# A LayerNorm between two halves of a projection: summing its squares once, and inside blocks of products

## The chip, the cores and the metric

The kernel runs on one core of a Trainium2 chip. Its time is the time of one execution on the device in microseconds (us). A core has a matrix engine (TensorE, PE in the profile; PEld is its weight load), VectorE (DVE), ScalarE (ACT), GpSimd (POOL) and SyncE (SP), each with a queue of instructions of its own that it works off in order, and DMA engines that move data beside them. Engines wait for each other through semaphores.

## The reference

One residual block over 512 positions of width 1024, in fp32:

```python
h = h + 0.5 * _swiglu(_rmsnorm(h, ffn1_norm[i]), ffn1_w_in[i], ffn1_w_out[i])
z = _rmsnorm(h, mix_norm[i]) @ w_in[i]
...
y_conv = _conv_module(conv_a, conv_gt, conv_w[i], conv_b[i], conv_ln_g[i], conv_ln_b[i])
y_gla = _gla(q, k, v, r, g_lr, gate_w_up[i], gate_b[i], gla_norm[i])
h = h + jnp.concatenate([y_conv, y_gla], axis=-1) @ w_out[i]
h = h + 0.5 * _swiglu(_rmsnorm(h, ffn2_norm[i]), ffn2_w_in[i], ffn2_w_out[i])
...
```

The convolution module multiplies `a` by sigmoid(`b`), runs a causal convolution of width 31 on each of 512 channels, and then normalizes over the channels:

```python
mu = jnp.mean(xf, axis=-1, keepdims=True)
var = jnp.mean(jnp.square(xf - mu), axis=-1, keepdims=True)
y = (xf - mu) * lax.rsqrt(var + EPS)
return (y * g.astype(jnp.float32) + b.astype(jnp.float32)).astype(x.dtype)
```

followed by SiLU. The change touches this LayerNorm and the product with `w_out` around it.

## The kernel before, in words

**Layout.** Activations lie transposed: 128 channels on the partitions, 512 positions along a row. The model's 1024 channels are eight such tiles `hT[0..7]`, the convolution's 512 channels four, `acc[0..3]` (named `cv` in the profile).

**Products.** An fp32 number is split into a high part of the type `F32R` and the rest, of the same type. A product of two such numbers is three matmuls, high by high, high by low, low by high (`mm3`, line 216). Weights come in by `load` (line 171, SyncE's queue) into one of two raw buffers (`wr`), and are split in one of two ways. `high` (line 178) casts the high part on ScalarE, and `low` (line 188) subtracts it from the raw weight on VectorE. `added` (line 193) does the low part without VectorE: its two lines are:

```python
act.mul(l3, r3, -1.0)
pool.dma_start(out=l3.bitcast(F32), in_=r3, accum_op=ALU.add)
```

Here `l3` and `r3` are the tiles that the profile names `wl` (or `wa`) and `wr`; the multiplication writes the negated weight rounded to the high part's precision, and a DMA issued from GpSimd's queue adds the raw weight to it. `wh` is the high part.

**The output projection.** It has eight blocks of 128 output channels, n = 0 to 7, and each block sums over eight input tiles `mix[k]`: k = 0 to 3 from the convolution (`yc`), k = 4 to 7 from the attention (`yg`). `first_part(n, w)` (line 882) does the twelve products of k = 4 to 7 of a block, which do not need the convolution; `part` (line 876) does either half. `part` can take a dictionary `mid` that calls a function ahead of the products of some k.

**The stretch that the change rewrites** (lines 945 to 979). Blocks 0 and 1 come first, then `taps(124)` issues what is left of the convolution's steps on VectorE (each multiplies a shifted row by a column of weights and adds it; with two tiles left, they alternate), then the last two weights, blocks 6 and 7, are split with `added`. Blocks 4 and 5 follow, then the last two of four products with the constant matrix `mean`, which put the mean over the channels into a PSUM tile `mub` (named `ax`). After block 2 VectorE subtracts the mean from each `acc[c]`, ScalarE squares it (`lnsq`), and 16 small products with a column of ones sum the squares of all four tiles into one column per 128 positions (`ax<-ones,lnsq`). `rsqrt_mean` (line 251) makes 1/sqrt of it with an operation `ms` on VectorE, a power on GpSimd, the optional function `between`, and four small operations on VectorE (`rs`). Block 3 follows; then `spread` (line 267) multiplies the columns with the identity so that the factor stands on all 128 partitions (`ax<-ident,rs`). Each tile is then multiplied by it on VectorE (`yc`), goes through SiLU with gain and bias on ScalarE, and is split by `split` (line 154): a cast on ScalarE (`ycH`), a subtraction on VectorE (`ycL`). Block 6 is issued last, and from there the loop over k adds the convolution's half to blocks 0 to 2, then to 3 to 6. Block 7 comes behind, and the second FFN.

**What sets the order.** All engine calls go through the class `Ordered` (line 36), so that nearly all instructions carry line 46 in the profile. While it is on, each of the three engines TensorE, VectorE and ScalarE gets its instructions in the order in which the code issues them; after `in_order(False)` a scheduler may move them. The stretch above is under the fixed order up to the loop over k. Raw buffers, PSUM banks (`bank`, seven; `aux`, one) and the tiles of `bt` come from pools that rotate; a new tile waits for the readers of the tile whose place it takes.

Of the kernel before, what the change touches and what calls it, by code (L numbers as in the profile page):

```python
# [8 lines left out]
F32 = mybir.dt.float32  # L9
# [6 lines left out]
P = 128  # L16
# [46 lines left out]
def block_kernel(ctx: ExitStack, tc: tile.TileContext, a: dict, out: bass.AP):  # L63
# [24 lines left out]
    def bt(dt=F32, s="a"):  # L88
        return big.tile([P, SEQ], dt, tag="A", bufs=NA, name=nm(s))
# [10 lines left out]
    def aux():  # L100
        return pp.tile([P, SEQ], F32, tag="aux", bufs=1, name=nm("ax"))
# [91 lines left out]
    def added(w):  # L193

        h3, l3, r3 = w
        act.mul(l3, r3, -1.0)
        pool.dma_start(out=l3.bitcast(F32), in_=r3, accum_op=ALU.add)
        return w
# [52 lines left out]
    def rsqrt_mean(ss, n, w, bufs=3, between=None):  # L251

        ms = tmp("ms", 16)[:, :w]
        dve.tensor_scalar(ms, ss, 1.0 / n, EPS, ALU.mult, ALU.add)
        r = tmp("rs0", 16)[:, :w]
        pool.tensor_tensor(out=r, in0=ms, in1=negh[:, :w], op=ALU.pow)
        if between is not None:
            between()
        t = tmp("rs1", 16)[:, :w]
        dve.tensor_tensor(out=t, in0=r, in1=r, op=ALU.mult)  # L260
        dve.tensor_tensor(out=t, in0=t, in1=ms, op=ALU.mult)
        dve.tensor_scalar(t, t, -0.5, 1.5, ALU.mult, ALU.add)
        rs = tmp(f"rs{bufs}", 16, bufs=bufs)[:, :w]
        dve.tensor_tensor(out=rs, in0=r, in1=t, op=ALU.mult)
        return rs
# [275 lines left out]
    def taps(n):  # L541

        for _ in range(n):
            if not conv:
                return
            i = turn[0] % min(2, len(conv))
            turn[0] += 1
            try:
                next(conv[i])
            except StopIteration:  # L550
                conv.pop(i)
# [317 lines left out]
    def ohigh(n):  # L869
        return (high4 if n in (4, 5) else high)(raw_o[n - n % 2][:, :, (n % 2) * P:(n % 2 + 1) * P])  # L870
# [5 lines left out]
    def part(ps, w, ks, first, last, mid={}):  # L876
        for k in ks:
            if k in mid:
                mid[k]()
            mm3(ps, *rows_of(w, k), *mix[k], first and k == ks[0], last and k == ks[-1])  # L880

    def first_part(n, w):
        ps = bank()
        part(ps, w, range(4, 8), True, False)
        half[n] = (w, ps)

    oload(0)
# [56 lines left out]
        nc.sync.dma_start(out=ptok[t], in_=a["p"][0, 0, t * P:(t + 1) * P, :])  # L944
    first_part(0, wo[0])
    first_part(1, wo[1])
    taps(124)
    for n in (6, 7):
        wo[n] = added(ohigh(n))
    first_part(4, wo[4])  # L950
    first_part(5, wo[5])
    for c in range(2, 4):
        pe.matmul(mub, mean, acc[c], start=False, stop=(c == 3))
    first_part(2, wo[2])
    sqs = []
    for c in range(4):
        dve.tensor_tensor(out=acc[c], in0=acc[c], in1=mub, op=ALU.subtract)
        sq = bt(s="lnsq")
        act.activation(sq, acc[c], AF.Square)
        sqs.append(sq)  # L960
    ssl = aux()[:, 0:TB]
    for c in range(4):
        for j in range(TB):
            pe.matmul(ssl[:, j:j + 1], sqs[c][:, j * P:(j + 1) * P], ones,
                      start=(c == j == 0), stop=(c == 3 and j == TB - 1), skip_group_check=True)
    rln = rsqrt_mean(ssl, D_CONV, TB)
    first_part(3, wo[3])
    rln = spread(rln, copy=False)
    yc = []
    for c in range(4):  # L970
        t = bt(s="yc")
        dve.tensor_tensor(out=t, in0=acc[c], in1=rln, op=ALU.mult)
        act.activation(t, t, AF.Silu, bias=vec("conv_ln_b", c), scale=vec("conv_ln_g", c))
        yc.append(t)
        if c == 2:
            mix[0] = split(yc[0], "yc")
    for c in range(1, 4):
        mix[c] = split(yc[c], "yc")
    first_part(6, wo[6])


    norm = Norm()
# [130 lines left out]
```

## Time and profile before

| | us |
|---|---|
| median of 3 runs | 998.3 (998.11 to 998.40) |
| profiled execution | 998.15 |
| its span in the trace | 996.4 |
| TensorE busy in the span | 978.2 (98%) |
| VectorE, ScalarE, GpSimd busy | 528.0, 355.4, 36.2 |
| mean granted clock of TensorE | 0.992 |

Times in the trace count from the start of the span. A row of the timeline gives start, length, engine, line, operation, output and inputs, the tile's shape, and how many such instructions it merges; in brackets stands how long the engine was idle before it, and for whom it waited. Matmuls overlap in a pipeline, so that a dense one is recorded with 0.39 us while the next starts 0.23 us later. A product of plain fp32 numbers (with `ones`, `ident` or `mean`) stands as two records.

### The profile page before, as it was taken

What the parts mean: (1) busy time and instruction counts of PE and PEld (TensorE: products, weight loads), DVE (VectorE), ACT (ScalarE), POOL (GpSimd) and SP (SyncE); (2) the same over time, 40 slices, a digit from 0 to 9 for tenths busy, and PEclk for the clock granted to TensorE, in tenths of its full rate; (3) what the DMA queues carried; (4) which work ended last, traced back from release to release, by engine and by line L of the source; (5) the groups of instructions that cost most, each with busy time, mean ns of one, the idle gap of its engine ahead of it and who ended that gap; (6) DMA issues with size and microseconds to landing.
All of it is one profiled execution on the core that took longest, in us unless ns stands there. A gap on an engine that the chain in (4) does not pass through costs nothing.

```text
span 996.4 us, 11226 instructions
## 1 busy us (share of the span) xinstructions
PE 978.2 (98%) x4594; PEld 807.1 (81%) x4594; DVE 528.0 (53%) x750; ACT 355.4 (36%) x541; POOL 36.2 (4%) x46
## 2 busy tenths in 40 slices
PE   7999999999999999999998999999999999999996
PEld 5888888888888888788877888888888888888885
DVE  4654334444434566999982844444333444345454
ACT  5633213232223343463654623322222232233442
POOL 1000000000000000001231000000000000000000
PEclk9999999999999999999997999999999999999998
DMA  5633223223422421125687223222233222233212
GB/s 171 196 125 107 85 86 118 93 85 105 149 85 80 131 85 43 42 85 128 128 130 144 78 99 121 85 83 87 95 116 127 87 85 80 69 100 111 85 43 85
DMA packets 99624, 100.53 MB, mean 101 GB/s; under 512 B 3331, under 2 KB 93013, under 8 KB 99572
## 3 DMA queue, kind: packets, MB, share of 16 engines
q1 hardware_dynamic: 90592, 93.93, 29.4%
q0 software_dynamic: 8800, 5.77, 4.5%
q8 instruction: 36, 0.59, 0.3%
q10 hardware_dynamic: 180, 0.12, 0.0%
q14 instruction: 16, 0.13, 0.0%
HBM read 92.46 MB, written 2.10 MB: 95 GB/s over the span
## 4 chain that ended last, share of the span: by engine, by line
PE 95%; DMA 2%; ACT 1%; SPq 0%; DVE 0%; issue 0%; POOLq 0%; DVEq 0%; ACTq 0%
PE ps L46 94%; PE ax L46 2%; DMA wr<-in_w_out 1%; DMA x<-in_x 1%; DMA wr<-in_ffn_w_in 0%; ACT wl L46 0%; ACT wh L46 0%; ACT ygH L46 0%; SPq L150 0%; ACT yc L46 0%; DVE yc L46 0%; ACT hgH L46 0%; POOLq L1109 0%; DVE m L46 0%; ACT lnsq L46 0%
## 5 line engine op out<-in xcount | busy, mean ns | idle before, releaser
L46 ACT CAST wh<-wr 128x1024 fp32r<-128x1024 f32 (+2 forms) x174 | 172.0, 992 | 452.6 <-PE ps L46 418.9
L46 PE MATMUL ps<-hgH,wh 128*128 128x512 f32 x752 | 293.4, 390 | 0.0
L46 PE MATMUL ps<-hgL,wh 128*128 128x512 f32 x752 | 292.9, 390 | 0.0
L46 PE MATMUL ps<-hgH,wl 128*128 128x512 f32 x752 | 292.9, 389 | 0.0
L46 DVE TENSOR_TENSOR wl<-wr,wh 128x1024 fp32r<-128x1024 f32 (+2 forms) x166 | 189.8, 1146 | 61.5 <-ACT wh L46 61.3
L46 PEld LDWEIGHTS ps<-hgH,wh 128*128 128x128 f32 x752 | 141.3, 188 | 29.9 <-issue 0.8
L46 PEld LDWEIGHTS ps<-hgH,wl 128*128 128x128 f32 x752 | 141.2, 188 | 29.3
L46 PEld LDWEIGHTS ps<-hgL,wh 128*128 128x128 f32 x752 | 141.3, 188 | 29.1
L46 PE MATMUL ps<-actL,wh 128*128 128x512 f32 x352 | 137.2, 390 | 0.0
L46 PE MATMUL ps<-actH,wl 128*128 128x512 f32 x352 | 137.1, 389 | 0.0
L46 PE MATMUL ps<-actH,wh 128*128 128x512 f32 x352 | 136.9, 389 | 0.0
L46 DVE TENSOR_TENSOR u<-ps,bc 128x512 f32<-128x512 f32 x48 | 33.2, 691 | 131.1 <-PE ps L46 131.1
L46 DVE SCALAR_TENSOR_TENSOR cv<-glu,cw,cv 128x504 f32<-128x504 f32 (+25 forms) x120 | 81.2, 732 | 0.6
L46 DVE TENSOR_TENSOR g<-ps,bc 128x512 f32<-128x512 f32 x48 | 33.1, 691 | 86.0 <-PE ps L46 83.1
L46 PEld LDWEIGHTS ps<-actL,wh 128*128 128x128 f32 x352 | 66.1, 188 | 13.9 <-DVE actL L46 0.2
L46 PEld LDWEIGHTS ps<-actH,wh 128*128 128x128 f32 x352 | 66.1, 188 | 13.7
L46 PEld LDWEIGHTS ps<-actH,wl 128*128 128x128 f32 x352 | 66.1, 188 | 13.6
L46 DVE SCALAR_TENSOR_TENSOR h<-ps,h 128x512 f32<-128x512 f32 x40 | 27.7, 692 | 89.1 <-PE ps L46 89.1
L46 PE MATMUL ps<-wh,hgH 128*128 128x512 f32 (+1 forms) x136 | 52.4, 385 | 0.0
L46 PE MATMUL ps<-wl,hgH 128*128 128x512 f32 (+1 forms) x136 | 51.8, 381 | 0.0
L46 PE MATMUL ps<-wh,hgL 128*128 128x512 f32 (+1 forms) x136 | 51.3, 377 | 0.0
L46 ACT ACTIVATE s<-g 128x512 f32<-128x512 f32 x48 | 30.3, 632 | 40.2 <-DVE g L46 35.5
(189 smaller groups left out, 783.8 us busy)
## 6 DMA issues: line engine op xcount, KB each, us to landing
wr<-in_ffn_w_in SPq DMA_DIRECT2D x42, 1024.0 KB, 5.1
wr<-in_w_in SPq DMA_DIRECT2D x10, 1024.0 KB, 5.0
wr<-in_ffn_w_out SPq DMA_DIRECT2D x12, 768.0 KB, 4.6
wr<-in_ffn_w_out SPq DMA_DIRECT2D x8, 1024.0 KB, 5.1
wr<-in_ffn_w_out SPq DMA_DIRECT2D x8, 640.0 KB, 6.8
wl<-wr POOLq DMA_DIRECT2D x8, 512.0 KB, 8.9
wr<-in_w_out SPq DMA_DIRECT2D x4, 1024.0 KB
wr<-in_ple_w_gate SPq DMA_DIRECT2D x8, 512.0 KB, 3.5
```

What stands on the lines that cost most here:

```text
L46: inst = call(*args, **kwargs)
```

## The change

It does five things in the stretch described. The rest of the convolution is issued tile by tile and no longer alternating. The last two products with `mean` stand apart, one behind block 4 and one behind block 5. The four squares are added on VectorE into one tile, and four products with the column of ones sum that. The weights of blocks 6 and 7 are cast behind the squares, and their low parts made by VectorE (`low`) and no longer by ScalarE and a DMA: that of block 6 while GpSimd computes the power, that of block 7 behind the last part of the convolution. The column sum stands inside block 3 (ahead of its products of k = 7), the spreading inside block 6 (at the same place), and each tile's SiLU is followed at once by its cast.

```diff
-    def first_part(n, w):
+    def first_part(n, w, mid={}):
         ps = bank()
-        part(ps, w, range(4, 8), True, False)
+        part(ps, w, range(4, 8), True, False, mid)
         half[n] = (w, ps)
...
     first_part(0, wo[0])
     first_part(1, wo[1])
-    taps(124)
-    for n in (6, 7):
-        wo[n] = added(ohigh(n))
+    for steps in list(conv):
+        for _ in steps:
+            pass
+    conv.clear()
     first_part(4, wo[4])
+    pe.matmul(mub, mean, acc[2], start=False, stop=False)
     first_part(5, wo[5])
-    for c in range(2, 4):
-        pe.matmul(mub, mean, acc[c], start=False, stop=(c == 3))
+    pe.matmul(mub, mean, acc[3], start=False, stop=True)
     first_part(2, wo[2])
-    sqs = []
+    sqs, lln, yc = [], [], []
     for c in range(4):
         dve.tensor_tensor(out=acc[c], in0=acc[c], in1=mub, op=ALU.subtract)
         sq = bt(s="lnsq")
         act.activation(sq, acc[c], AF.Square)
         sqs.append(sq)
-    ssl = aux()[:, 0:TB]
-    for c in range(4):
-        for j in range(TB):
-            pe.matmul(ssl[:, j:j + 1], sqs[c][:, j * P:(j + 1) * P], ones,
-                      start=(c == j == 0), stop=(c == 3 and j == TB - 1), skip_group_check=True)
-    rln = rsqrt_mean(ssl, D_CONV, TB)
-    first_part(3, wo[3])
-    rln = spread(rln, copy=False)
-    yc = []
-    for c in range(4):
-        t = bt(s="yc")
-        dve.tensor_tensor(out=t, in0=acc[c], in1=rln, op=ALU.mult)
-        act.activation(t, t, AF.Silu, bias=vec("conv_ln_b", c), scale=vec("conv_ln_g", c))
-        yc.append(t)
-        if c == 2:
-            mix[0] = split(yc[0], "yc")
+    for n in (6, 7):
+        wo[n] = ohigh(n)
+
     for c in range(1, 4):
-        mix[c] = split(yc[c], "yc")
-    first_part(6, wo[6])
+        dve.tensor_tensor(out=sqs[0], in0=sqs[0], in1=sqs[c], op=ALU.add)
+
+    def ln_sums():
+        lln.append(rsqrt_mean(colsum([sqs[0]]), D_CONV, TB, between=lambda: low(wo[6])))
+
+    def ln_out():
+        rln = spread(lln[0], copy=False)
+        for c in range(5):
+            if c < 4:
+                t, hi, lo = bt(s="yc"), bt(F32R, "ycH"), bt(F32R, "ycL")
+                dve.tensor_tensor(out=t, in0=acc[c], in1=rln, op=ALU.mult)
+                act.activation(t, t, AF.Silu, bias=vec("conv_ln_b", c), scale=vec("conv_ln_g", c))
+                act.copy(hi, t)
+                mix[c] = hi, lo
+                yc.append(t)
+            if c:
+                hi, lo = mix[c - 1]
+                dve.tensor_tensor(out=lo, in0=yc[c - 1], in1=hi.bitcast(F32), op=ALU.subtract)
+        low(wo[7])
+
+    first_part(3, wo[3], {7: ln_sums})
+    first_part(6, wo[6], {7: ln_out})
```

The order of instructions shows it at three places. The first is ScalarE between the weights of block 3 (`wh_3885`, `wl_3886`) and the SiLUs (`yc`), before:

```order
L46 CAST wh_3885<-wr_3729 128x1024
L46 ACTIVATE wl_3886<-wr_3729 128x1024
L46 CAST wh_3936<-wr_3890 128x1024
L46 ACTIVATE wl_3937<-wr_3890 128x1024
L46 CAST wh_3941<-wr_3890 128x1024
L46 ACTIVATE wl_3942<-wr_3890 128x1024
L46 ACTIVATE lnsq_3988<-cv_2667 128x512
L46 ACTIVATE lnsq_3991<-cv_2668 128x512
L46 ACTIVATE lnsq_3994<-cv_2669 128x512
L46 ACTIVATE lnsq_3997<-cv_2670 128x512
L46 ACTIVATE yc_4044<-yc_4044,vcol 128x512
L46 ACTIVATE yc_4047<-yc_4047,vcol 128x512
```

and of the change:

```order
L46 CAST wh_3885<-wr_3729 128x1024
L46 ACTIVATE wl_3886<-wr_3729 128x1024
L46 ACTIVATE lnsq_3978<-cv_2667 128x512
L46 ACTIVATE lnsq_3981<-cv_2668 128x512
L46 ACTIVATE lnsq_3984<-cv_2669 128x512
L46 ACTIVATE lnsq_3987<-cv_2670 128x512
L46 CAST wh_3989<-wr_3890 128x1024
L46 CAST wh_3992<-wr_3890 128x1024
L46 ACTIVATE yc_4042<-yc_4042,vcol 128x512
L46 CAST ycH_4043<-yc_4042 128x512
L46 ACTIVATE yc_4048<-yc_4048,vcol 128x512
```

The four instructions on raw buffer `wr_3890` (blocks 6 and 7) have become two and stand behind the squares, and each SiLU has its cast behind it. The second place is TensorE from the last products of block 2 (`ps_3974` before, `ps_3964` in the change) to the start of block 3 (`ps_4026`, `ps_3998`), before:

```order
L46 MATMUL ps_3974<-ygL_3878,wh_3880 128x512
L46 MATMUL ps_3974<-ygH_3876,wl_3881 128x512
L46 MATMUL ax_3999<-ones,lnsq_3988 128x1 x4
L46 MATMUL ax_3999<-ones,lnsq_3991 128x1 x4
L46 MATMUL ax_3999<-ones,lnsq_3994 128x1 x4
L46 MATMUL ax_3999<-ones,lnsq_3997 128x1 x4
L46 MATMUL ps_4026<-ygH_3864,wh_3885 128x512
L46 MATMUL ps_4026<-ygL_3866,wh_3885 128x512
L46 MATMUL ps_4026<-ygH_3864,wl_3886 128x512
```

and of the change:

```order
L46 MATMUL ps_3964<-ygH_3876,wl_3881 128x512
L46 MATMUL ps_3998<-ygH_3864,wh_3885 128x512
L46 MATMUL ps_3998<-ygL_3866,wh_3885 128x512
L46 MATMUL ps_3998<-ygH_3864,wl_3886 128x512
L46 MATMUL ps_3998<-ygH_3868,wh_3885 128x512
L46 MATMUL ps_3998<-ygL_3870,wh_3885 128x512
L46 MATMUL ps_3998<-ygH_3868,wl_3886 128x512
L46 MATMUL ps_3998<-ygH_3872,wh_3885 128x512
L46 MATMUL ps_3998<-ygL_3874,wh_3885 128x512
L46 MATMUL ps_3998<-ygH_3872,wl_3886 128x512
L46 MATMUL ax_4008<-ones,lnsq_3978 128x1 x4
L46 MATMUL ps_3998<-ygH_3876,wh_3885 128x512
```

Block 3 now follows block 2 directly, with its low weight `wl_3886` in the third product, and the column sum stands behind nine of its products. The third place is VectorE from the end of the additions of squares to the first multiplication by the factor, in the change alone (before, the five small operations stood without the split between them):

```order
L46 TENSOR_TENSOR lnsq_3978<-lnsq_3978,lnsq_3987 128x512
L46 TENSOR_SCALAR ms_4013<-ax_4008 128x4
L46 TENSOR_TENSOR wl_3990<-wr_3890,wh_3989 128x1024
L46 TENSOR_TENSOR rs_704_4018<-rs_703_4015 128x4
L46 TENSOR_TENSOR rs_704_4018<-rs_704_4018,ms_4013 128x4
L46 TENSOR_SCALAR rs_704_4018<-rs_704_4018 128x4
L46 TENSOR_TENSOR rs_705_4022<-rs_703_4015,rs_704_4018 128x4
L46 TENSOR_TENSOR yc_4042<-cv_2667,ax_4037 128x512
```

The split of block 6's weight (`wl_3990`) stands behind `ms`, which reads the column sum, and ahead of the four operations that finish the factor.

## The prediction

> **What bounds the kernel now.** I read the page first (TensorE busy 98% of the 996.4 us), then the chain of work that ended last. From 542 us on it is TensorE alone up to the tail; around the change, from 512 to 542 us, it leaves TensorE:
>
> ```profile
> 512.66 9.47 DMA wr<-in_w_out
> ...
> 522.15 0.75 ACT wh L46
> ...
> 523.11 1.05 ACT wl L46
> 524.16 0.93 ACT wh L46
> 525.09 0.96 ACT wl L46
> 526.05 0.53 ACT lnsq L46
> ...
> 526.62 6.99 PE ax L46 x32
> 533.61 4.34 PE ps L46 x12
> 537.95 0.91 PE ax L46 x8
> ...
> 538.88 0.70 DVE yc L46
> ...
> 541.83 0.52 ACT ycH L46
> ...
> 542.39 19.35 PE ps L46 x84
> ...
> 585.14 0.79 PE ax L46 x8
> ...
> 591.01 345.26 PE ps L46 x1525
> ```
>
> Columns are start, length, what. Four ScalarE instructions on the last output weights (`wh`, `wl`, 522.15 to 526.05), which waited for their DMA, stand ahead of the squares `lnsq`. The 16 column-sum products (32 records, two each) then take 6.99 us; four of the same kind later take 0.79 us. A dense product costs 19.35/84 = 0.230 us. I call 542.39, where the first product with the convolution's result (`ycH`) starts, H0: behind it TensorE waits for nothing until the tail, so what moves H0 moves the end. TensorE's timeline and stretches of 1 us (columns: stretch, length, busy time of PE, PEld, DVE, ACT, POOL, granted clock, DMA share, GB/s):
>
> ```profile
> 519.05 1.88 PE L46 MATMUL ax<-cv,mean 128*128 128x512 f32 x4
> ...
> 523.31 0.39 PE L46 MATMUL ps<-ygH,wl 128*128 128x512 f32 x1
> 526.62 6.99 PE L46 MATMUL ax<-ones,lnsq 128*128 128x1 f32 x32 [2.93 <-ACT lnsq L46]
> ...
> 534.47 0.63 PE L46 MATMUL ps<-ygH,wl 128*128 128x512 f32 x1
> 534.89 0.63 PE L46 MATMUL ps<-ygH,wh 128*128 128x512 f32 x1
> ```
>
> ```profile
> 526.00:527.00 1.00, 0.38 (x2) 0.38 (x2) 0.00 (x0) 1.00 (x4) 0.56 (x1) 0.72 0.41 46
> 527.00:528.00 1.00, 1.00 (x6) 1.00 (x6) 0.00 (x0) 1.00 (x3) 1.00 (x1) 0.50 1.28 143
> ...
> 536.00:537.00 1.00, 1.00 (x4) 0.77 (x4) 0.00 (x0) 0.00 (x0) 0.00 (x0) 0.67 1.38 174
> ...
> 988.00:989.00 1.00, 0.41 (x4) 0.20 (x2) 0.55 (x3) 0.55 (x2) 0.00 (x0) 1.00 0.39 150
> ...
> 990.00:991.00 1.00, 0.00 (x0) 0.00 (x0) 0.50 (x2) 0.44 (x2) 0.23 (x1) 0.82 0.00 0
> ```
>
> TensorE idles 2.93 us, and its clock falls to 0.50 at 526.44 (a share of 0.72 means 0.44 us of full speed in that microsecond) and is back at 536.66 (share 0.67). While it is down a dense product costs 0.42 to 0.43 (534.47 to 534.89) and a column-sum record 6.99/32 = 0.218 instead of 0.79/8 = 0.099. In the tail the last product ends at 988.41 and the clock falls at 990.64. The distances, 10.22 and 453.98 us, are 3 and 133 steps of 3.41 us, so I take the clock to be decided on that grid: 523.03, 526.44, 529.85, 533.27, 536.68. The windows in which it fell held TensorE work of about 0.7 of 3.41 us (to the end of the product at 523.31) and, in the tail, 988.41 - 987.23 = 1.2. Column sums did not bring it back; one window of dense products (533.27 to 536.68) did.
>
> **The change, part by part.** *One sum instead of four, at full clock:* 16 products become 4. *Squares ahead of the weights:* the subtractions of the mean start at 520.97, as before; the mean's products are only spread between two blocks, and convolution block 3 still ends at 519.00, ahead of them:
>
> ```profile
> 510.03 8.97 DVE L46 SCALAR_TENSOR_TENSOR cv<-glu,cw,cv 128x510 f32<-128x510 f32 x12
> 520.97 2.48 DVE L46 TENSOR_TENSOR cv<-cv,ax 128x512 f32<-128x512 f32 x4 [1.96 <-PE ax L46]
> 533.64 0.16 DVE L46 TENSOR_SCALAR ms<-ax 128x4 f32<-128x4 f32 x1 [10.20 <-PE ax L46]
> ...
> 534.96 0.16 DVE L46 TENSOR_TENSOR rs<-rs 128x4 f32<-128x4 f32 x1 [1.15 <-POOL rs L256]
> ...
> 535.56 0.16 DVE L46 TENSOR_TENSOR rs<-rs,rs 128x4 f32<-128x4 f32 x1
> ...
> 554.88 0.68 DVE L46 TENSOR_TENSOR sqacc<-sqacc,sq 128x512 f32<-128x512 f32 x1
> ...
> 558.75 1.22 DVE L46 TENSOR_TENSOR wl<-wr,wh 128x1024 fp32r<-128x1024 f32 x1
> ```
>
> ```profile
> 522.15 1.05 ACT L46 CAST wh<-wr 128x1024 fp32r<-128x1024 f32 x1 [9.27 <-DMA wr<-in_w_out]
> ...
> 525.96 2.17 ACT L46 ACTIVATE lnsq<-cv 128x512 f32<-128x512 f32 x4
> ...
> 543.69 0.82 ACT L46 ACTIVATE yc<-yc,vcol 128x512 f32<-128x512 f32 x1 [1.36 <-DVE yc L46]
> ```
>
> ScalarE was idle for 9.27 us before 522.15, so each square (2.17/4 = 0.54) follows its subtraction (2.48/4 = 0.62), the last ends at 524.1. The three added additions on VectorE (0.68 each, like `sqacc`, of which some 0.6 is the step) end at 523.45 + 1.9 = 525.35. ScalarE casts `wh` of blocks 6 and 7 behind the squares, 524.1 to 526.1, with the raw load there since 522.13. The two `wl` multiplications and two GpSimd DMAs go away; two splits of 1.22 us on VectorE take their place.
>
> *What is late next.* With the sums ready at 525.35, TensorE comes to block 3 at 523.54, right behind block 2, ten microseconds sooner than before (533.61). Its third product reads `wl` of block 3, and that weight is still built by an accumulating DMA:
>
> ```profile
> 513.17 1.55 POOL L197 DMA_DIRECT2D wl<-wr  x1 [0.34 <-ACT wl L46]
> ```
>
> ```profile
> wl<-wr POOLq DMA_DIRECT2D x1, 512.0 KB, 13.2
> ...
> wl<-wr POOLq DMA_DIRECT2D x1, 512.0 KB, 12.2
> ```
>
> ```profile
> 526.52 12.64 SPq L174 DMA_DIRECT2D wr<-in_ffn_w_in  x2
> ```
>
> This DMA (the first landing row) lands 13.2 us after its issue, at 526.4; SyncE's next load, which needs the raw buffer it reads, is issued at 526.52 and confirms it. Nothing that the change removes ran on the queues before: the two DMAs that go away follow the `wl` multiplications, which ended at 524.16 and 526.05. So the new order meets a wait that lay hidden: TensorE does two products, to 524.0, and idles until 526.45. This is an order in TensorE's queue, so block 3's other products and the column sum behind them wait too. The price: 2.45 us of idle where 2.93 stood. For a bound, the next such DMA took 12.2 us (second landing row), 1.0 us less; 13.2 was the longest of those around, so I take no later end.
>
> *The clock.* On the grid, window 523.03 to 526.44 would hold 1.0 to 1.1 us of TensorE work, between the two that let the clock fall (0.7 and 1.2). I take it that it falls again, at 526.44, and comes back at 529.85 since that window is filled by dense products (seven at 0.43 = 3.0 us).
>
> *The sum.* Seven products at 0.427 from 526.45: 529.44. Column sum: two records at 0.218, at 529.85 the clock returns, six at 0.10: 530.47. Three products of block 3 and two of block 6: 531.6. The third product of block 6 needs its `wl`: that split stands on VectorE behind `ms`, which waits for the column sum, so it runs from 530.66 (0.16 + hand-over) to 531.90; TensorE loses 0.35. The power on GpSimd runs beside the split (533.80 to 534.96 with its hand-overs before); the four small `rs` operations are queued behind the split, 0.8 us (534.96 to 535.72 before), ready at 532.7 and hidden. Seven products more: 531.95 + 1.6 = 533.54. Spreading (0.91, as at 537.95): 534.45. From there to H0: multiplication 0.70, SiLU 0.82, cast 0.60 (0.52 in the chain and its start-up), 0.15 of hand-overs (0.02 to 0.05 between rows) = 2.27 against 3.54 before (538.85 to 542.39), where three SiLUs went ahead of the first cast. H0 = 536.72, of which 0.69 is covered by block 6's last three products.
>
> 542.39 - 536.72 = 5.67 us gained. Behind H0 the convolution's next parts are needed after nine to twelve products each, 2.1 us or more apart, and made every 1.4 (a multiplication and a subtraction on VectorE, a SiLU and a cast on ScalarE), so no further wait; block 7's split is done some 6 us after H0 and used behind the 84 products, 19 us after. Profiled execution 998.15 us (span 996.4 and 1.75 around it), 0.15 under the median of the runs: 998.15 - 5.67 = 992.5.
>
> **Rivals.** *A2, a second fall.* In 533.27 to 536.68 TensorE would idle 1.6 us and spend 0.9 in spreading; if that counts as too little work, the next 3.41 us run at half speed: +1.7, 994.2. For it: small products did not lift the clock before. Against: 1.8 of 3.41 us is more work than in either window that let it fall.
>
> *B, the clock holds* through the 2.45 us gap. Seven products 1.6, sum 0.79, five products to 529.96, split done at 530.3, seven products, spreading, 2.27: H0 = 535.07, gain 7.3, 990.8. For it: the gap is shorter than the one that let the clock fall, and if the grid lies elsewhere against the kernel's start, the gap is cut in two. Against: the tail, where it fell 2.2 us after the last product. The Trainium skill ("TensorE: Matmul & The Clock Gate", the section "Why this matters for your kernels") speaks for B: it asks to avoid idle gaps over about 3 us and lets the clock drop after a whole window of idling, so by that rule this gap is harmless and the time is that of B. The trace disagrees with it in part: 2.93 us were enough here.
>
> *C, block 3's weight is there in time.* No gap: nine products to 525.6, sum to 526.4, split to 527.8, H0 = 532.6, gain 9.8, 988.4. Against: the landing row, and the SyncE row that confirms it.
>
> *D, slower: the clock falls at 526.44 and small products keep it down.* All steps at half clock: 529.4, sum 531.2, block 3 and 6 to 536.3, spreading 1.8, H0 = 540.4. From there each microsecond at half speed loses 0.5, so it decides if the clock is still down at 544.4; on the grid it would return at 546.9, 2.0 - 3.25 = -1.25, 999.4. Against: one dense window brought it back before.
>
> *E, no change:* the second FFN's first loads come late and take the gain back. The raw buffer of blocks 6 and 7 is now freed by VectorE's last split, about 542.5, where the DMA freed it by 539.2 (the end of the SyncE row, whose second load waited for it); that load serves the second FFN, which TensorE reaches only behind the 84 products and block 7. About 998. Nothing in the waits speaks for it.
>
> **How the numbers follow.** A 0.45, A2 0.17, B 0.22, C 0.10, D 0.03, E 0.03. The predicted time is A's, 992.5. Low end: B with the DMA at its 12.2 us, 990.8 - 1.0 = 989.8; high end: A2 with the 0.2 by which runs differ, 994.4. C, D and E (0.16) lie outside. A measurement of this kernel can tell about 0.2% (2 us) from no change: A, A2, B and C are beyond that, so faster 0.94, same 0.03 (E), slower 0.03 (D).
>
> **What would show it.** Right: in the changed profile TensorE's wait sits before the third product of block 3, ends about 526.4 and is put down to a DMA or to nothing that fits; the squares end about 524.1; four sums instead of sixteen; clock 0.50 for about 3.4 us from 526.4; H0 near 536.7. Wrong: no gap at 524 (C), a clock of 1.00 throughout (B), a second stretch of 0.50 after 536 (A2), or H0 earlier with the end unmoved (E).

## The result, and the profile after

| | before | changed |
|---|---|---|
| median of 5 executions, us | 998.11 (997.65 to 998.4) | 992.21 (991.64 to 994.8) |
| ratio, 95% interval | | 0.9949 [0.9934, 0.9965] |
| profiled execution, us | 998.15 | 994.39 |
| its span, us | 996.4 | 992.7 |
| its H0, us | 542.39 | 538.47 |

The kernel became faster by 0.5%, and the interval of the ratio lies below 1. The times of the changed kernel do not lie around their median: three are between 991.6 and 992.3 and two at 994.4 and 994.8. The profiled execution is one of the two longer ones, so the page shows the change at its worst.

The page's count of engine time, of the changed kernel (columns: engine, busy us, share of the span, instructions):

```profile
PE 974.0 (98%) x4570; PEld 802.3 (81%) x4570; DVE 532.7 (54%) x755; ACT 354.8 (36%) x539; POOL 33.7 (3%) x44
```

TensorE is as full as before, and this says nothing of where 4 us went. The chain that ended last, of the changed kernel, does (columns: start, length, what):

```profile
513.14 13.40 DMA wl<-wr
...
526.59 2.59 PE ps L46 x7
529.17 1.50 PE ax L46 x8
530.67 4.63 PE ps L46 x12
535.30 0.91 PE ax L46 x8
...
536.23 0.70 DVE yc L46
...
536.95 0.82 ACT yc L46
...
537.80 0.63 ACT ycH L46
...
538.47 19.35 PE ps L46 x84
```

Before, the chain ran over a load, four ScalarE instructions on weights (two casts, two multiplications) and a square into 32 records of column sums. Now it runs over the accumulating DMA that builds block 3's low weight, into seven products of that block, and the sum has eight records. The squares and the weights of blocks 6 and 7 are no longer in it. From the spreading (0.91) on, one SiLU stands ahead of the cast, and the steps have the lengths that the prediction took for them (0.70, 0.82, and 0.63 for 0.60). TensorE's timeline of the changed kernel shows the wait (columns: start, time from the first record's start to the last one's end, what, and in brackets the idle time before it and what ended it):

```profile
523.69 0.39 PE L46 MATMUL ps<-ygL,wh 128*128 128x512 f32 x1
526.59 0.50 PE L46 MATMUL ps<-ygH,wl 128*128 128x512 f32 x1 [2.51 <-DMA wl<-wr]
...
528.97 1.70 PE L46 MATMUL ax<-ones,lnsq 128*128 128x1 f32 x8
```

and its stretches of 1 us show the clock (columns as in the prediction):

```profile
526.00:527.00 1.00, 0.41 (x2) 0.37 (x3) 0.00 (x0) 0.00 (x0) 0.00 (x0) 1.00 0.00 0
527.00:528.00 1.00, 1.00 (x5) 0.81 (x4) 0.00 (x0) 0.00 (x0) 0.00 (x0) 0.76 0.11 20
528.00:529.00 1.00, 1.00 (x4) 0.71 (x4) 0.00 (x0) 0.00 (x0) 0.00 (x0) 0.50 0.80 250
...
534.00:535.00 1.00, 1.00 (x5) 0.78 (x4) 0.00 (x0) 0.00 (x0) 0.00 (x0) 0.83 0.00 0
```

A share of 0.76 puts the fall at 527.52, one of 0.83 the return at 534.34: 6.82 us, two steps of 3.41, where before there were three (526.44 to 536.66). The fall comes when TensorE is already at work again, 1.1 us later than the grid of the profile before has it.

The engines that feed it, in the changed kernel, ScalarE first:

```profile
521.65 2.43 ACT L46 ACTIVATE lnsq<-cv 128x512 f32<-128x512 f32 x4 [8.81 <-DVE cv L46]
523.99 1.98 ACT L46 CAST wh<-wr 128x1024 fp32r<-128x1024 f32 x2
```

```profile
523.33 2.28 DVE L46 TENSOR_TENSOR lnsq<-lnsq,lnsq 128x512 f32<-128x512 f32 x3
...
530.79 1.23 DVE L46 TENSOR_TENSOR wl<-wr,wh 128x1024 fp32r<-128x1024 f32 x1
532.94 0.16 DVE L46 TENSOR_TENSOR rs<-rs 128x4 f32<-128x4 f32 x1 [0.93 <-POOL rs L256]
```

```profile
530.96 1.95 POOL L256 TENSOR_TENSOR rs<-ms,negh 128x4 f32<-128x4 f32 x1 [16.27 <-DVE ms L46]
```

The squares end at 524.08 and their additions at 525.61, three microseconds before the sum starts, so the sum does not wait for them. GpSimd's power takes 1.95 us beside VectorE's split, and the first `rs` operation waits 0.93 us for it.

### The profile page after: what moved, and what is told of

Read it like the earlier page. It is cut to its first block, busy times and chain, and to the rows that moved or that the text cites. A ratio compares the mean times of both kernels' runs of the same rounds, so it can differ in the third digit from the quotient of the medians.

```text
span 992.7 us, 11176 instructions
## 1 busy us (share of the span) xinstructions
PE 974.0 (98%) x4570; PEld 802.3 (81%) x4570; DVE 532.7 (54%) x755; ACT 354.8 (36%) x539; POOL 33.7 (3%) x44
## 4 chain that ended last, share of the span: by engine, by line
PE 96%; DMA 2%; ACT 1%; DVE 0%; SPq 0%; issue 0%; POOLq 0%; DVEq 0%; ACTq 0%
PE ps L46 95%; DMA wl<-wr 1%; PE ax L46 1%; DMA wr<-in_ffn_w_in 0%; ACT ygH L46 0%; ACT wl L46 0%; ACT wh L46 0%; SPq L150 0%; ACT yc L46 0%; DVE yc L46 0%; ACT hgH L46 0%; POOLq L1117 0%; ACT ycH L46 0%; ACT wa L46 0%; DVE m L46 0%
## 5 line engine op out<-in xcount | busy, mean ns | idle before, releaser
L46 DVE TENSOR_TENSOR wl<-wr,wh 128x1024 fp32r<-128x1024 f32 (+2 forms) x168 | 192.3, 1147 | 61.6 <-ACT wh L46 61.5
```

The lines of the kernel that those rows point to most:

```text
L46: inst = call(*args, **kwargs)
```

## The experiments

Three questions: is the wait on block 3's weight what remains, and is the clock part of its price; what is each part of the change worth; and what does the kernel gain when both findings are used. Intervals are those of the ratio to the kernel before, on the same chip; its median there was 997.5 to 997.8. All kernels compute the whole result.

**again.** The changed kernel, unaltered, for the spread of its times.

> The changed kernel, unchanged, five more times. The five times of the result lie in two groups, 991.6 to 992.2 with a mean granted clock of 0.998 and 994.4 to 994.8 with 0.994 to 0.995. Theory W (the gap in front of block 3's third product, and a clock that falls in it in some executions only, as the 3.41 us grid happens to lie against the kernel's start): again two groups, about 991.9 and 994.5, the clock 0.003 to 0.004 lower in the slower one; in a profile of the faster group the gap of 2.5 us stands at 524 as before, the clock stays 1.00 from 520 to 545, and H0 is near 536. Rival S (the groups come from something else, such as the time the DMAs take): the profile of the faster group has a shorter gap.

Measured: 993.03, 993.08, 994.52, 992.39 and 992.56, ratio 0.9957 [0.9945, 0.9969]. With the five above, ten executions sort by their mean granted clock: 0.998 in five (991.64 to 992.56), 0.996 in two (993.03 and 993.08), 0.994 or 0.995 in three (994.39, 994.52, 994.80). The profiled one here is of 993.08; its chain, TensorE row and clock:

```profile
512.42 14.05 DMA wl<-wr
...
526.51 3.31 PE ps L46 x7
529.83 0.80 PE ax L46 x8
...
532.01 1.91 PE ps L46 x7
533.92 1.02 PE ax L46 x8
...
537.20 8.01 PE ps L46 x34
```

```profile
526.51 0.80 PE L46 MATMUL ps<-ygH,wl 128*128 128x512 f32 x1 [3.18 <-DMA wl<-wr]
```

```profile
526.00:527.00 1.00, 0.48 (x1) 0.49 (x2) 0.00 (x0) 0.00 (x0) 0.00 (x0) 0.62 0.01 1
...
529.00:530.00 1.00, 1.00 (x7) 0.81 (x6) 0.00 (x0) 0.00 (x0) 0.00 (x0) 0.68 1.05 369
```

Here the clock falls at 526.24 and returns at 529.64: one step, the course of case A, with H0 at 537.20. TensorE comes to the wait 0.7 us sooner than in the profile after and the DMA lands at the same time, so the wait is longer, 3.18 us for 2.51. The same program thus has its clock fall for two steps or for one, and the edge lies at 527.52 in one profile and at 526.24 in the other. That it does not fall at all in five executions is read from their mean clock of 0.998 alone; none of them was profiled, and the expectation had no group at 993.

**lowlast.** Block 3's eight products with the high weights go first, then the sum, then the four with the low weights:

```diff
-    first_part(3, wo[3], {7: ln_sums})
+    ps = bank()
+    for k in range(4, 8):
+        wh, wl = rows_of(wo[3], k)
+        pe.matmul(ps, wh, mix[k][0], start=(k == 4), stop=False)
+        pe.matmul(ps, wh, mix[k][1], start=False, stop=False)
+    ln_sums()
+    for k in range(4, 8):
+        pe.matmul(ps, rows_of(wo[3], k)[1], mix[k][0], start=False, stop=False)
+    half[3] = (wo[3], ps)
```

> The changed kernel, with the products of block 3 in another order: the eight with its high weight first, then the column sum, then the four with its low weight. No DMA and no other engine is touched. Theory W: eight products end at 525.4, the sum runs from 525.65 (the added squares end at 525.6) to 526.45, and the low products find their DMA landed at 526.5: gap 0.3 us where 2.5 stood, the clock never falls, H0 at 532.8 and a time of 988.5, all executions within 0.5 us. Rival S (the landing is not what cost the time): 991.9 as before, or two groups still.

Measured: 988.79 (988.45 to 990.87), ratio 0.9918 [0.9905, 0.9931], 4.2 us under "again" on the same chip by the medians (3.9 by the ratios). TensorE's rows of this kernel:

```profile
524.99 1.05 PE L46 MATMUL ax<-ones,lnsq 128*128 128x1 f32 x8 [0.22 <-DVE lnsq L46]
...
532.63 0.50 PE L46 MATMUL ps<-ycH,wh 128*128 128x512 f32 x1 [1.58 <-ACT ycH L46]
```

The sum starts as soon as the squares are added, with 0.22 us of idle where there were 2.51, and H0 is at 532.63. Without the wait the time is that of case C (988.4), so the wait and the fall of the clock behind it are what stood between the changed kernel and that time. One of the four executions, 990.87, has a clock of 0.996; where it fell there was not traced.

**dvelow3.** The same wait taken away at the other end: VectorE makes block 3's low weight and no DMA does.

```diff
-    for n in (2, 3):
-        wo[n] = added(ohigh(n))
+    wo[2] = added(ohigh(2))
+    wo[3] = ohigh(3)
...
     conv.clear()
+    low(wo[3])
```

> The changed kernel, with the low part of block 3's weight made by VectorE (1.22 us, behind the convolution, where VectorE was idle 1.7 us before the subtractions) and no longer by ScalarE and a DMA. Theory W: no gap at 524, nine products to 525.6, sum to 526.45, H0 at 532.7, 988.4, one group. Rival V (VectorE becomes the bound): the split delays the subtractions, they start after 520.93, and what is gained at the gap is lost there: 990 or more.

Measured: 988.9 (988.24 to 989.28), ratio 0.9914 [0.9901, 0.9927]. TensorE goes from block 2 through block 3 into the sum without idling, in its chain:

```profile
520.51 4.77 PE ps L46 x21
525.29 1.06 PE ax L46 x8
```

Two edits that have nothing in common but the weight's lateness bring the same time, so the remaining wait was for that weight. The split costs VectorE nothing here: it fills an idle time, and the subtractions of the mean start at 520.55.

**sumfirst.** Whether it is the order or the gap that counts: the sum ahead of all of block 3, which leaves a gap of 2 us for the squares, with no DMA in it.

```diff
-    first_part(3, wo[3], {7: ln_sums})
+    ln_sums()
+    first_part(3, wo[3])
```

> The changed kernel, with the column sum ahead of all products of block 3. TensorE then idles from 523.5 to 525.65 for the added squares on VectorE, 2.1 us, and for no DMA. Without a fall of the clock: sum to 526.45, twelve products to 529.2, block 6 behind them without a wait for its split, H0 at 534.4, 990.1. Theory W with the grid: a gap of 2.1 us still fills over half of a 3.41 us window in about half of the executions, so part of them fall to half clock and take 1.7 to 3.4 us longer, two groups. Rival H (only a wait for a DMA, or a gap over 2.4 us, lets the clock fall): one group at 990.

Measured: 990.25, 991.29, 991.36, 992.2 and 992.33, ratio 0.9941 [0.9928, 0.9954] (a sixth execution took 2,543 us and is left out). The sum's row:

```profile
526.27 1.05 PE L46 MATMUL ax<-ones,lnsq 128*128 128x1 f32 x8 [2.03 <-DVE lnsq L46]
```

The two times above 992 have a mean clock of 0.996, the three others 0.998 or 0.999, and the profiled one (991.29) kept its clock through the gap. By the mean clocks, then, no DMA is needed for the fall, and some 2.0 us of idle time do it in some executions and not in others; an execution of sumfirst with a fall was not profiled.

**weightsfirst and lowlast_wf.** What the early squares are worth, with the remaining wait in place and without it: the casts of blocks 6 and 7 again ahead of the squares, in the changed kernel and in lowlast.

```diff
     sqs, lln, yc = [], [], []
+    for n in (6, 7):
+        wo[n] = ohigh(n)
     for c in range(4):
...
         sqs.append(sq)
-    for n in (6, 7):
-        wo[n] = ohigh(n)
-
```

> The changed kernel, with ScalarE's two casts for blocks 6 and 7 back ahead of the squares, where they wait for their load until 522.15. The squares then end at 526.4 and the added squares at 527.0, where 524.1 and 525.6 stood. Theory W: block 3's seventh product behind the landed DMA ends at 528.1 or later, so the sum is still ready in time and this part of the change is worth nothing as the change stands: 992 to 993.1, as before. Rival Q (the squares' place is what the gain comes from): 2 us slower or more, 994 to 995.

> The version with the low-weight products of block 3 last, with ScalarE's casts for blocks 6 and 7 back ahead of the squares. With the gap in front of block 3's weight the squares' place showed no cost in the trace, since the sum stood behind the gap. Without the gap TensorE reaches the sum at 525, and the added squares end at 527.2 instead of 525.0: H0 2.2 us later, 991.0, with an idle time of 2.2 us in which the clock falls in some executions. Rival: the squares' place does not matter here either, 988.8.

Measured: weightsfirst 994.18 (992.15 to 995.19), ratio 0.9964 [0.9952, 0.9977], an interval that overlaps that of "again"; lowlast_wf 993.23 (992.36 to 994.07), 0.9958 [0.9946, 0.997], where lowlast had 0.9918. VectorE's and TensorE's rows of weightsfirst:

```profile
525.51 2.28 DVE L46 TENSOR_TENSOR lnsq<-lnsq,lnsq 128x512 f32<-128x512 f32 x3 [1.93 <-ACT lnsq L46]
```

```profile
527.54 0.50 PE L46 MATMUL ps<-ygH,wl 128*128 128x512 f32 x1 [3.29 <-DMA wl<-wr]
```

and TensorE's of lowlast_wf:

```profile
528.53 1.05 PE L46 MATMUL ax<-ones,lnsq 128*128 128x1 f32 x8 [2.34 <-DVE lnsq L46]
```

The median of weightsfirst is the figure of rival Q (994 to 995), not the 992 to 993.1 expected, but its trace is that of the expectation: the squares are added up at 527.8, while TensorE is held by the DMA to 527.5 and then has seven products to do, so the squares' place lies beside another wait. In lowlast_wf nothing covers it, TensorE idles 2.34 us for the squares, and the clock falls for one step (529.54 to 532.96). Its time is 2.2 us above the 991.0 expected: all five executions have a mean clock of 0.995 or 0.996, and the profiled one comes to block 0's first product at 508.15, 1.4 us later than lowlast's (506.74), ahead of anything that the edit touches. Four of weightsfirst's five executions have a clock of 0.994, against three of ten in the changed kernel; whether that is its later gap or chance, five executions can't tell.

**squaresonly and onesumonly.** Two parts of the change by themselves, on the kernel before. The first moves the weights of blocks 6 and 7 behind the squares and keeps their DMAs, the second only adds the squares up for one sum.

```diff
     taps(124)
-    for n in (6, 7):
-        wo[n] = added(ohigh(n))
     first_part(4, wo[4])
...
         sqs.append(sq)
+    for n in (6, 7):
+        wo[n] = added(ohigh(n))
```

```diff
-    ssl = aux()[:, 0:TB]
-    for c in range(4):
-        for j in range(TB):
-            pe.matmul(ssl[:, j:j + 1], sqs[c][:, j * P:(j + 1) * P], ones,
-                      start=(c == j == 0), stop=(c == 3 and j == TB - 1), skip_group_check=True)
+    for c in range(1, 4):
+        dve.tensor_tensor(out=sqs[0], in0=sqs[0], in1=sqs[c], op=ALU.add)
+    ssl = colsum([sqs[0]])
```

> The kernel before, with one part of the change: the weights of blocks 6 and 7 are split behind the squares, with ScalarE and the DMA as before; 16 sums, and the sum and the spreading between the blocks. The squares end at 524.1, TensorE does the 16 sums without a gap and at full clock, 523.5 to 526.7, block 3 to 529.5 (its weight landed at 526.5), spreading to 530.5; then block 6 waits for its low weight as in the run above, 534 to 538, and the products with the convolution's parts stand behind it: H0 at 537 to 540, 993 to 997. Theory W: the gain of the early squares is real, and most of it goes to the wait of block 6, put down to a DMA in the trace. Rival Q (early squares alone give the gain): 992 or less.

> The kernel before, with one part of the change: the four squares added on VectorE and summed by four products, between blocks 2 and 3 as before. The squares still end at 528.1, the additions at 528.8, and TensorE idles from 523.7 to 528.9, 5 us instead of 2.9, at half clock from about 526.5 on. Four products at half clock take 1.75, so block 3 starts at 530.6 instead of 533.6, and H0 moves by 3.0 if block 3 still runs at half clock: 995. Rival: the clock stays down longer, since the dense window begins where it began before or the longer idle time adds one; 996.5.

Measured: squaresonly 993.53 (993.12 to 996.64), ratio 0.9965 [0.9955, 0.9976], 4.2 us under before by the medians and 3.5 by the ratio, in which its two executions above 996 count; onesumonly 996.29 (994.99 to 997.28), 0.9987 [0.9978, 0.9995], 1.2 us under it. Onesumonly came out at the figure of its rival (996.5): TensorE idles 6.08 us for the squares, and the clock is down to 536.88, behind all of block 3. In squaresonly TensorE has one wait left in this stretch, and it is again an accumulating DMA, now block 6's:

```profile
535.50 0.50 PE L46 MATMUL ps<-ygH,wl 128*128 128x512 f32 x1 [2.02 <-DMA wl<-wr]
```

Its cause is in GpSimd's rows (two DMA issues in one row), below the power that belongs to the LayerNorm's factor:

```profile
527.34 1.03 POOL L256 TENSOR_TENSOR rs<-ms,negh 128x4 f32<-128x4 f32 x1 [13.81 <-DVE ms L46]
528.34 3.18 POOL L197 DMA_DIRECT2D wl<-wr  x2
```

The sums of squaresonly follow block 2 without idle time from 522.36, and yet the clock falls at 524.84 and stays down for two steps:

```profile
524.00:525.00 1.00, 1.00 (x11) 1.00 (x10) 0.00 (x0) 1.00 (x2) 0.00 (x0) 0.92 0.18 32
```

**dma67.** The change with the low weights of blocks 6 and 7 built as before, by ScalarE and a DMA:

```diff
     for n in (6, 7):
-        wo[n] = ohigh(n)
+        wo[n] = added(ohigh(n))
...
-        lln.append(rsqrt_mean(colsum([sqs[0]]), D_CONV, TB, between=lambda: low(wo[6])))
+        lln.append(rsqrt_mean(colsum([sqs[0]]), D_CONV, TB))
...
-        low(wo[7])
```

> The changed kernel, with the low parts of blocks 6 and 7 made by ScalarE and a DMA as before, behind the squares. Both theories expect a new wait: ScalarE's multiplication for block 6 ends at 526.1, the DMA lands 8 to 12 us later (7.9 and 12.2 in the profile of before), 534 to 538, and block 6's third product, with the spreading and H0 behind it in TensorE's queue, waits for it: H0 at 539 to 543, 995 to 999, all of the gain or most of it gone. If the landing takes the 7.9 us and the clock returns in time, 995; rival N (the DMA lands before TensorE needs it): 992.6.

Measured: 1001.56 (1000.34 to 1003.02), ratio 1.0038 [1.0024, 1.0051]: slower than before, and above all that was expected. The expectation had the two DMAs leave when their source was ready. In GpSimd's queue they stand behind the power, which waits for the sum, which waits for block 3's DMA. The kernel's code calls them ahead of the power, but GpSimd is not among the three engines whose order is fixed, and the built program has the power first; their sources, ScalarE's multiplications, ended at 525.59 and 527.49. GpSimd's and TensorE's rows of this kernel:

```profile
530.82 1.03 POOL L256 TENSOR_TENSOR rs<-ms,negh 128x4 f32<-128x4 f32 x1 [16.49 <-DVE ms L46]
531.81 3.18 POOL L197 DMA_DIRECT2D wl<-wr  x2
```

```profile
538.96 0.79 PE L46 MATMUL ps<-ygH,wl 128*128 128x512 f32 x1 [6.09 <-DMA wl<-wr]
```

TensorE idles 6.09 us for block 6's weight, the clock is down from 526.90 to 543.96, five steps, and H0 is at 546.30. So with GpSimd's queue in this order VectorE's split of blocks 6 and 7 is no small item: without it the rest of the change loses. What the DMAs would cost ahead of the power was not run.

**splitlate.** The SiLUs and the split in the order of before, the rest as changed:

```diff
-        for c in range(5):
+        for c in range(4):
...
-                t, hi, lo = bt(s="yc"), bt(F32R, "ycH"), bt(F32R, "ycL")
+                t = bt(s="yc")
...
-                act.copy(hi, t)
-                mix[c] = hi, lo
...
-            if c:
-                hi, lo = mix[c - 1]
-                dve.tensor_tensor(out=lo, in0=yc[c - 1], in1=hi.bitcast(F32), op=ALU.subtract)
+                if c == 2:
+                    mix[0] = split(yc[0], "yc")
+        for c in range(1, 4):
+            mix[c] = split(yc[c], "yc")
```

> The changed kernel, with the convolution's parts split as before (three SiLUs ahead of the first cast). Working of the prediction: from the end of the spreading to H0 3.54 us again in place of 2.27, +1.3, 994.2; TensorE's idle time in front of H0 grows from 1.6 to 2.9 us, so that the clock falls there in most executions and 1.7 us more are lost, up to 996. Rival: the SiLUs are hidden anyway, 992.6.

Measured: 995.88 (993.58 to 997.68), ratio 0.998 [0.9971, 0.9989]. In its chain two more SiLUs (1.50 us) stand between the first and the cast:

```profile
535.84 0.70 DVE yc L46
...
536.57 0.61 ACT yc L46
...
537.28 1.50 ACT yc L46 x2
538.79 0.52 ACT ycH L46
```

From the end of the spreading (535.82) to H0 (539.35) are 3.53 us, in the change 2.27 (536.20 to 538.47): 1.26 us by the path. By the ratios the part is worth 2.3 to 3.1 us (0.9980 less 0.9957, and less 0.9949, of 997.6). The rest is not the fall ahead of H0 that was expected, as far as the trace goes: TensorE idles 2.85 us there and the clock stays at 1.00. It was down from 527.32 to 534.14, as in the profile of the changed kernel. Of the eleven executions eight have a mean clock of 0.993 to 0.995, of the changed kernel's ten three; whether that is the edit or chance stays open.

**sixteen.** The change with its sixteen sums as before, inside block 3:

```diff
-    for c in range(1, 4):
-        dve.tensor_tensor(out=sqs[0], in0=sqs[0], in1=sqs[c], op=ALU.add)
-
     def ln_sums():
-        lln.append(rsqrt_mean(colsum([sqs[0]]), D_CONV, TB, between=lambda: low(wo[6])))
+        ssl = aux()[:, 0:TB]
+        for c in range(4):
+            for j in range(TB):
+                pe.matmul(ssl[:, j:j + 1], sqs[c][:, j * P:(j + 1) * P], ones,
+                          start=(c == j == 0), stop=(c == 3 and j == TB - 1), skip_group_check=True)
+        lln.append(rsqrt_mean(ssl, D_CONV, TB, between=lambda: low(wo[6])))
```

> The changed kernel with the 16 sums in place of the additions and four sums, at the same place inside block 3. Working of the prediction: at full clock 16 products take 3.2 us where four take 0.8, +2.4; at half clock 7.0 where four take 1.75, +5.2. The additions that go away were ready ahead of the sum and give nothing back. Executions in which the clock does not fall: 994.5; those in which it falls, in which the sums also keep it down longer: 997 to 1000. Rival: the sums hide the factor's chain or the split of block 6's weight, and the time moves by less than 1 us.

Measured: 997.43 (994.6 to 1001.22, twelve executions), ratio 0.9999 [0.9987, 1.0012]: the change's whole gain is gone. Five executions lie between 994.6 and 995.5, seven between 997.3 and 1001.2 at clocks of 0.991 to 0.993. The expectation took a group near 994.5 for executions in which the clock holds. The profiled one (995.53) is of the faster group and has the sums at full clock, but the clock falls behind them:

```profile
528.47 3.63 PE L46 MATMUL ax<-ones,lnsq 128*128 128x1 f32 x32
```

```profile
531.00:532.00 1.00, 1.00 (x11) 1.00 (x11) 0.00 (x0) 0.00 (x0) 0.00 (x0) 1.00 0.25 84
...
533.00:534.00 1.00, 1.00 (x4) 0.70 (x3) 0.44 (x1) 0.00 (x0) 1.00 (x1) 0.50 0.01 2
```

TensorE was idle at no time between 526.75 and the end of the spreading here, and yet the clock is at 0.50 at 533 (it fell at 532.61): the step of 3.41 us before that held column sums to 532.10 and 0.5 us of dense products, and the clock fell as if the sums were none.

**both.** The two findings together: lowlast, block 6 in the same order with the spreading ahead of its seventh high product, and block 6's split behind the `rs` operations.

```diff
-        lln.append(rsqrt_mean(colsum([sqs[0]]), D_CONV, TB, between=lambda: low(wo[6])))
+        lln.append(rsqrt_mean(colsum([sqs[0]]), D_CONV, TB))
+        low(wo[6])
...
+        if k == 7:
+            ln_out()
+        wh, wl = rows_of(wo[6], k)
+        pe.matmul(ps, wh, mix[k][0], start=(k == 4), stop=False)
+        pe.matmul(ps, wh, mix[k][1], start=False, stop=False)
+    for k in range(4, 8):
+        pe.matmul(ps, rows_of(wo[6], k)[1], mix[k][0], start=False, stop=False)
```

> The version with the low-weight products of block 3 last, with two more edits: block 6 in the same way (eight high-weight products, with the spreading ahead of the seventh, then four low ones), and the split of block 6's weight on VectorE behind the four small operations of the factor and no longer beside GpSimd's power. In all profiles so far the power takes 1.95 us where VectorE's 1.23 us split runs beside it, and 1.03 us in the kernel before, where VectorE was idle. Theory: the power takes 1.0 again, the factor is ready 2.1 us after ms instead of 3.0, the spreading starts at 528.3 instead of 529.3, H0 at 531.8 instead of 532.6, 988.0. Rival: the power takes 1.9 whatever runs beside it, and TensorE waits for the factor: 988.8 as without the edits.

Measured: 988.1 (987.82 to 988.77), ratio 0.9909 [0.9895, 0.9923], faster than the kernel before and the changed one: 9.4 us under before by the medians. GpSimd's and TensorE's rows:

```profile
526.56 1.03 POOL L256 TENSOR_TENSOR rs<-ms,negh 128x4 f32<-128x4 f32 x1 [12.32 <-DVE ms L46]
```

```profile
531.95 0.50 PE L46 MATMUL ps<-ycH,wh 128*128 128x512 f32 x1 [0.89 <-ACT ycH L46]
```

The power is back at 1.03 us with no split beside it, and TensorE idles 0.89 us ahead of H0. Against lowlast alone H0 is 0.68 us earlier in the profiles; the two intervals overlap.

## Why the prediction was right, and where it was right by luck

**The bound.** H0 sets the end: from H0 to the end of the profiled execution are 455.76 us before, 455.92 in the change, and between 455.63 and 455.93 in the traces of the twelve experiments. No later load takes anything back, so E is out, and a time less 455.9 us is an H0.

**The new wait.** It is where the prediction put it, ahead of block 3's third product: 2.51 us for 2.45. The DMA landed 13.40 us after its issue (14.05 in "again") for 13.2; "no later end" was thus a little short. The squares ended at 524.08 for 524.1, their additions at 525.61 for 525.35. Lowlast and dvelow3 show that this wait, with its clock, is what keeps the change from case C's 988.4: they have 988.8 and 988.9.

**The clock.** Here a step failed: "I take the clock to be decided on that grid". Falls begin at 526.44, 527.52 and 526.24 in three profiles, all with steps of 3.41 us: the step holds, the place against the kernel's start does not. Hence the gap (2.51 and 3.18 us in the two profiles) lies sometimes mostly within one window and is sometimes cut by an edge, which B had named. By their mean clocks, of ten executions the clock held in five (B, given 0.22), fell for one step in two (A, 0.45) and for two in three. The two-step ones, at 994.4 to 994.8, have A2's time, but the one that was profiled not its course: no second fall after 536, but a single fall that the window with the column sum in it did not end. Two of the ten lie above the range's end of 994.4. The Trainium skill ("TensorE: Matmul & The Clock Gate", the section "Why this matters for your kernels") asks to avoid gaps over about 3 us; by that rule the clock would have held behind the 2.51 us of the profile after, and it fell; behind the 3.18 us of "again" it fell as well.

**The sizes.** B was worked out as 990.8 and came as 991.64 to 992.56, H0 of 535.7 to 536.7 for 535.07. The sum takes 1.05 us at full clock for 0.79 (lowlast), seven products behind the split 1.91 for 1.6 and the spreading 1.02 for 0.91 ("again"): 0.7 together, and 991.5. The rest, up to 1.0, stays open, as no execution of that kind was profiled. A later landing may be part of it: in the six traces that have this wait it ends between 526.18 (splitlate) and 527.54 (weightsfirst), where B has 526.45. A was 992.5 and came as 993.05. So the median, 992.21, is an execution of case B that met A's figure because B was 1.4 us too quick on paper: the direction and the main mechanism were earned; that the median lies within 0.3 us of the forecast is luck.

**The power.** "The power on GpSimd runs beside the split" was right about the place and wrong about the price, which it had at nothing: the power took 1.95 us beside the split against 1.03 alone (both, dma67), and the first `rs` operation was 0.93 us late for it. It stayed hidden behind block 6's products. The profile before has the pair already, at 586 us, and I had not read it:

```profile
586.04 1.22 DVE L46 TENSOR_TENSOR wl<-wr,wh 128x1024 fp32r<-128x1024 f32 x1
```

```profile
586.27 1.86 POOL L256 TENSOR_TENSOR rs<-ms,negh 128x4 f32<-128x4 f32 x1 [51.34 <-DVE ms L46]
```

The Trainium skill ("SBUF — State Buffer", the section "SBUF: two separate sides") has VectorE's operations with two inputs from SBUF and GpSimd's exclude each other on a shared port; these durations agree with that, 0.9 us of waiting within 1.2.

**The parts.** Split at once: 1.27 us of path forecast (3.54 less 2.27), 1.26 measured. The parts do not add up. The early squares alone bring 3.5 (by the ratio) to 4.2 us (by the medians) on the kernel before, where the sum stood right behind the last block and waited for them. Inside the change the DMA's wait covers them in the trace of weightsfirst. With that wait gone they are worth something again: lowlast_wf lies 4.0 us (ratios) to 4.4 us (medians) above lowlast, of which the traces show 2.1 us of idle time (2.34 less 0.22) and one step of the clock; up to 1.4 may be where the profiled execution happened to stand before the stretch. One sum alone brings 1.2, inside the change 4.2 to 5.0 (0.9999 less 0.9957, and less 0.9949, of 997.5). Of these some 2.4 are the sums' own length at full clock (3.47 us in the chain of sixteen, 1.05 in that of lowlast); the rest fits the lower mean clocks of sixteen.

## What to carry to other kernels

When a block of work is moved forward into a gap, list its operands with the time that each is there: the first one that lay hidden is the next wait, and within the block the products that need it can go last. A gap of 2 to 3 us in front of TensorE has no single price while its clock's windows drift against the program; work out each case, take many executions, and close the gap rather than guess which case it is. On a queue that computes and issues transfers, a transfer behind a waiting computation is as late as that computation; where a scheduler orders that queue, look at the order in the built program and not in the code.

## What the runs showed of the hardware

- The clock changes in steps of 3.41 us that are not tied to the kernel's start: it was down for 3.40 us ("again"), 6.82 (the changed kernel), 10.22 (before) and 17.06 (dma67), from 526.24, 527.52, 526.44 and 526.90. One kernel has groups of times, 991.6 to 992.6, 993.05 and 994.4 to 994.8; falls of one and of two steps were seen in its traces, and that the fastest group has no fall is read from its mean clock.
- An idle time's length alone does not decide it. The clock fell behind 2.34 us (lowlast_wf), 2.51 (the changed kernel), 2.64 (splitlate) and 3.18 ("again"), and held through 2.03 (sumfirst), 2.16 (sixteen) and 2.85 (splitlate, ahead of H0). Counted on each trace's own steps, and without the column sums, a step at whose end it fell held 1.14 us of products at most in this stretch (splitlate, 523.91 to 527.32) and 1.55 in the tail (squaresonly, 982.23 to the last product's end at 983.78); the emptiest step found through which it held had 1.61 (splitlate, 537.55 to 540.96). The case of A2, 1.8 us of work of which the spreading is 0.9, stands in squaresonly (531.68 to 535.09), and there the clock held.
- Products of one moving column seem to count for little or nothing to the clock: behind 3.63 us of them, without idle time in that step, it fell (sixteen); it fell while they ran behind a dense block without idle time (squaresonly, 524.84); and with 1.7 us of them in a step it did not return (the profile after).
- A GpSimd operation on 128x4 elements took 1.03 us alone and 1.95 us beside a VectorE subtraction of 1.23 us with two inputs in SBUF.
- An accumulating DMA of 512 KB took 13.04 (sixteen) to 14.17 us (weightsfirst) for block 3 in the experiments, and 7.11 us for block 6 where it was issued late, in dma67's chain:

```profile
531.81 7.11 DMA wl<-wr
```
